# Summing the modulation vectors: from ones-matmuls and transposes on TensorE to block transposes and row sums on VectorE

## The chip, the cores and the metric

The kernel runs on one core of a Trainium2 chip. The metric is device time in microseconds (us), the median of several executions. The engines named below are TensorE (PE, with its weight loads as PEld), VectorE (DVE), ScalarE (ACT), GpSimd (POOL) and SyncE (SP), which here issues all the transfers from HBM.

## The reference, cut to what matters

Two layers of a diffusion backbone over 256 latent tokens and 256 context tokens, width 1024. Each layer is modulated by six vectors of 1024 numbers for each of the two streams (latent and context). They come from a product of one vector with a wide matrix:

```python
mod   = silu(c)     @ w_mod[l] + b_mod[l]      # (6144,) for the latent stream
mod_c = silu(c_ctx) @ w_mod[l] + b_mod[l]      # (6144,) for the context stream
sh1, sc1, gt1, sh2, sc2, gt2 = split(mod, 6)
h = rms_norm(x, g_norm1) * (1 + sc1) + sh1     # -> w_in, gates, attention, convolution, Fourier mixing
x = x + gt1 * merge_branches(...)              # -> w_o
x = x + gt2 * sq_relu_mlp(rms_norm(x, g_norm2) * (1 + sc2) + sh2)
```

The second layer leaves the context stream after its keys and values, so it needs two vectors of `mod_c` there and six of `mod`. Everything is float32.

## The kernel before, in words

Activations lie with the 1024 features on partitions (`xT`, 8 tiles of 128 features by 512 tokens). Every weight matrix is streamed from HBM once, in chunks of 1 MB (`raw`, two buffers), and each half chunk is split into a high part (`whi`, a cast on ACT, L384) and a low part (`wlo`, a subtraction on DVE, L385). Three matmuls then make one product of float32 accuracy (L473, L476, L478 in `fm`). The stages are named in the tiles: `init`, `n1L`, `uL`, `convL`, `fouL`, `qkvL`, `gateL`, `agL`, `woL`, `ffL`, once for each layer.

Beside this main work runs a side stream, the modulation vectors. For each of the six vectors and each half of it (512 columns, `j` and `h`), `mod_loads` fetches four transfers of 512 KB (`modr`, two buffers, L298), and `mod_steps` accumulates on DVE: `acc[p, n] = sum over k of cs[p, k] * w[128 k + p, n]`, one multiply (L349) and seven multiply-adds (L351) of 128x512 for each stream. What is left is the sum over the 128 partitions `p`, a turn of the 512 sums from a row onto partitions (the modulation is used as `modT[p, f]`, feature `128 f + p`), and the bias. That is `mod_finish`, called once for each pair of accumulators: two streams of one half vector, or two halves of one vector where only one stream is needed. There are 8 calls for layer 0 and 8 for layer 1, 16 in all.

`mod_steps` is a generator. Each `yield` in it is a step, and `fm` calls `mods.tick()` after each contraction tile, which takes 0.6, 1.3, 0.4 or 0.8 steps by stage (`RATES`). `mod_need` takes steps until a vector is ready, and `mods.drain()` takes all that are left before the end of layer 0. In `mod_finish` the steps `W1` and `W2` are pauses, so that the next instruction of the chain is written some tiles later. The final order on each engine is set by a scheduler, which simulates the program and places each instruction where its inputs are ready; instructions in `tc.keep_in_program_order` keep their order among themselves. All engines are in order once the program is built, so a late instruction holds what is behind it on its engine.

In the kernel before, a call does four matmuls with `ones` as weights of 32 columns, each on 256 columns of an accumulator and each into its own group of 32 partitions of one PSUM tile (L308), a copy on ACT (L313), two transposes of 128x128 on TensorE through a PSUM tile of the shared pool `aux` (L318), and two additions of the bias on DVE (L321).

Of the kernel before, what the change touches and what calls it, by code (L numbers as in the profile page):

```python
# [8 lines left out]
F32 = mybir.dt.float32  # L9
F32R = mybir.dt.float32r  # L10
AF = mybir.ActivationFunctionType
ALU = mybir.AluOpType
AX = mybir.AxisListType
PSUM = bass.MemoryType.PSUM

P = 128
# [14 lines left out]
W_INIT, W_RMS = 6, 6  # L31
MLAG = 1
LAG = 2
W1, W2 = 3, 2
RATES = [0.6, 1.3, 0.4, 0.8]
AR = [1.3, 0.8]

# [2 lines left out]
def hybrid_block_kernel(  # L40
# [7 lines left out]
    nc = tc.nc  # L48
    V = nc.vector
    A = nc.scalar  # L50
    G = nc.gpsimd
    PE = nc.tensor

    const = ctx.enter_context(tc.tile_pool(name="const", bufs=1))
# [7 lines left out]
    pmod = ctx.enter_context(tc.tile_pool(name="pmod", bufs=1, space=PSUM))  # L62
# [4 lines left out]
    def nm(s):  # L67
        uid[0] += 1
        return f"{stage[0]}_{s}_{uid[0]}"
# [4 lines left out]
    def scratch(shape=(P, 512), dt=F32):  # L74
        return scr.tile(list(shape), dt, tag="scr", name=nm("scr"))

    def small(shape, tag, dt=F32, bufs=4):
        return tiny.tile(shape, dt, tag=tag, name=nm(tag), bufs=bufs)

    def bank(shape=(P, 512)):  # L80
        return psum.tile(list(shape), F32, tag="mm", name=nm("mm"))

    def aux(shape=(P, 512)):
        return paux.tile(list(shape), F32, tag="aux", name=nm("aux"))
# [45 lines left out]
    ident = const.tile([P, P], F32, tag="ident", name="ident")  # L130
    make_identity(nc, ident)
    ones = const.tile([P, P], F32, tag="ones", name="ones")
    G.memset(ones, 1.0)
    mhalf = const.tile([P, 1], F32, tag="mhalf", name="mhalf")
    G.memset(mhalf, -0.5)
    cT = scratch((P, KT, 32))
# [10 lines left out]
    prm = []  # L147
# [38 lines left out]
    def accs(streams):  # L186
        t = const.tile([P, 4, 512], F32, tag="kT", name=nm("acc"))[:, 0, :]
        return [Acc(s * S, S, t) for s in streams]
# [62 lines left out]
    modT = [const.tile([P, 48, 2], F32, tag=f"modT{l}", name=f"modT{l}") for l in range(DEPTH)]  # L251
# [49 lines left out]

    def mod_finish(accs, dsts, l):

        ps = pmod.tile([P, 256], F32, tag="mod", name=nm("mod"))
        for _ in range(W1):
            yield
        for g in range(4):
            tc.keep_in_program_order(PE.matmul(  # L308
                ps[32 * g : 32 * g + 32, :], ones[:, 0:32],
                accs[g // 2][:, (g % 2) * 256 : (g % 2 + 1) * 256], start=True, stop=True,  # L310
            ))
        sb = scratch()[:, :256]
        A.copy(sb, ps)  # L313
        for _ in range(W2):
            yield
        tp = aux((P, 2, P))
        for e in range(2):
            tc.keep_in_program_order(PE.transpose(tp[:, e, :], sb[:, e * P : (e + 1) * P], ident))  # L318
        tv = tp.rearrange("p e (g r) -> p g e r", r=32)[:, :, :, 0]
        for i, (f, s) in enumerate(dsts):  # L320
            V.tensor_tensor(  # L321
                modT[l][:, f : f + 4, s].rearrange("p (g e) -> p g e", e=2),
                tv[:, 2 * i : 2 * i + 2, :],
                prm[l][:, f : f + 4].rearrange("p (g e) -> p g e", e=2), op=ALU.add,
            )
        yield

    ready = set()
# [5 lines left out]
    def mod_steps(todo):  # L334
        loads = mod_loads(todo)
        cur = next(loads, None)
        accs, dsts = [], []
        while cur is not None:
            l, j, ns, h, k2, r = cur
            cur = next(loads, None)  # L340
            if k2 == 0:
                for s in range(ns):
                    accs.append(small([P, 512], "acc", bufs=2))
                    dsts.append((j * 8 + h * 4, s))
            for kk in range(2):
                for s in range(ns):
                    a, w = accs[s - ns], cs2[:, s, 2 * k2 + kk : 2 * k2 + kk + 1]
                    if k2 + kk == 0:
                        v = V.tensor_scalar(a, r[:, kk, :], w, None, op0=ALU.mult)  # L349
                    else:  # L350
                        v = V.scalar_tensor_tensor(a, r[:, kk, :], w, a, op0=ALU.mult, op1=ALU.add)  # L351
                    tc.keep_in_program_order(v)
                    yield
            if k2 == KT // 2 - 1 and len(accs) == 2:
                yield from mod_finish(accs, dsts, l)
                accs, dsts = [], []
                if h == 1:
                    ready.add((l, j))
# [187 lines left out]
    for l in range(DEPTH):  # L546
# [69 lines left out]
        for ft in range(2):  # L616
            t = scratch()
# [15 lines left out]
        for ft in range(2):  # L633
# [4 lines left out]
            t = scratch()  # L638
# [31 lines left out]
        for tt in range(nt):  # L670
            ps = aux((P, 2, 256))
# [17 lines left out]
        for ft in range(2):  # L689
            ps = aux()  # L690
# [111 lines left out]
        for ci, c0 in ((2, OFF_K), (0, OFF_Q), (1, OFF_Q + 256)):  # L802
            ch = plain(w_in[l], 0, c0, (V, G) if last else (V, V)).prep()
            for tt in range(4 if ci == 2 else nt):
                ps = bank((P, 256))
                tk = slice(tt * P, (tt + 1) * P)
                for kt in range(KT):
                    wh, wl = ch.at(kt, 0, 256)
                    a, b = hh[:, kt, tk], hl[:, kt, tk]
# [122 lines left out]
        for j in range(4):  # L932
# [5 lines left out]
            for o in range(2):  # L938
                f = 2 * j + o
# [42 lines left out]
        acc = accs(streams)  # L982
# [50 lines left out]
        for b in range(nblk):  # L1033
            subs = []
            hot = None
            for q in range(2):
                hid = bigt([P, 2, per, T])
                subs.append(hid)
                for j in range(per // 2):
# [12 lines left out]
                    for o in range(2):  # L1052
                        t = scratch()[:, :T]
# [20 lines left out]
            if nr == 1:  # L1074
                if final and not last:
                    mods.drain()
                    acc = accs(streams)
# [17 lines left out]
            else:  # L1095

                nk = 2 * per
                for h in range(2):
# [14 lines left out]
                    for tt in range(2):  # L1113
                        t = scratch()
# [51 lines left out]
```

## Time and profile before

| what | value |
|---|---|
| median of 3 runs | 1146.95 us (1144.39 to 1149.06) |
| profiled execution: its time, its span | 1148.35 us, 1146.5 us |
| PE busy | 1127.0 us, 98% |
| DVE busy | 779.6 us, 68% |
| ACT busy | 504.4 us, 44% |
| DMA, over the span | 180 MB, 156 GB/s |
| granted TensorE clock | 0.996 of full speed |

Durations are those of one profiled execution. A PE row's time is that of one matmul from its start to its modelled end; matmuls overlap, so what a matmul costs is read from the distance between the starts around it. A float32 matmul that isn't split by the program shows as two records. The stages that hold the side stream lie between 131 us and 747 us of the span: `gateL` of layer 0 from about 131 us, `agL` from 285 us, `woL` from about 346 us, `ffL` from about 398 us.

### The profile page before, as it was taken

To read this page: it belongs to the slowest core of one execution; us is meant where nothing else is said; L and a number is where in the kernel's file an instruction comes from. 1 tells how busy PE (TensorE), PEld (TensorE's weight loads), DVE (VectorE), ACT (ScalarE), POOL (GpSimd) and SP (SyncE) were. 2 spreads that over 40 slices of the span, in tenths; PEclk is the share of its full clock that TensorE was granted. 3 is DMA by queue.
4 is the path that set the end of the run, shared out by engine and by line. 5 is a ranking of instruction groups with operands and counts; after the bars stand their busy time and mean duration, and the time that the engine had idled before them with its cause. 6 is when DMAs were issued, how large, how long until landed. Compare 5 with 4: busy or idle time off the path is not lost.

```text
span 1146.5 us, 17789 instructions
## 1 busy us (share of the span) xinstructions
PE 1127.0 (98%) x7075; PEld 983.9 (86%) x7075; DVE 779.6 (68%) x1444; ACT 504.4 (44%) x896; POOL 50.6 (4%) x54
## 2 busy tenths in 40 slices
PE   7899999999999999999999999999999999999998
PEld 6689887887787998878888888899999999988986
DVE  4577775568878876766746664778886567756754
ACT  4345544443332454143134135244666456754752
POOL 0002100000000100000000000043300000000000
PEclk9999999999999999999999999999999999999999
DMA  9933322225655243655456664515434465656653
GB/s 279 295 97 100 107 78 92 82 85 147 202 175 179 91 162 117 196 184 165 146 168 202 217 209 145 199 61 175 139 111 129 131 207 178 184 182 186 184 184 111
DMA packets 156796, 180.03 MB, mean 157 GB/s; under 512 B 5260, under 2 KB 126504, under 8 KB 156712
## 3 DMA queue, kind: packets, MB, share of 16 engines
q1 hardware_dynamic: 156712, 178.88, 50.1%
q8 instruction: 56, 0.92, 0.3%
q14 instruction: 28, 0.23, 0.1%
HBM read 177.81 MB, written 1.05 MB: 156 GB/s over the span
## 4 chain that ended last, share of the span: by engine, by line
PE 88%; DVE 4%; DMA 4%; SPq 2%; ACT 1%; issue 1%; POOL 1%; DVEq 0%; ACTq 0%; POOLq 0%
PE ffL_mm L473 12%; PE ffL_mm L476 12%; PE ffL_mm L478 12%; PE gateL_mm L478 5%; PE gateL_mm L473 5%; PE gateL_mm L476 5%; PE agL_mm L476 3%; PE agL_mm L473 3%; PE agL_mm L478 3%; PE ffL_mm L1112 3%; PE ffL_mm L1111 3%; PE ffL_mm L1110 3%; PE woL_mm L476 2%; PE woL_mm L478 2%; PE woL_mm L473 2%; SPq L105 2%
## 5 line engine op out<-in xcount | busy, mean ns | idle before, releaser
L384 ACT CAST ffL_whi<-ffL_raw 128x1024 fp32r<-128x1024 f32 x128 | 134.4, 1052 | 218.9 <-PE ffL_mm L478 164.3
L385 DVE TENSOR_TENSOR ffL_wlo<-ffL_raw,ffL_whi 128x1024 fp32r<-128x1024 f32 x127 | 155.0, 1222 | 99.3 <-ACT ffL_whi L384 99.1
L473 PE MATMUL ffL_mm<-woL_big,ffL_whi 128*128 128x258 f32 (+2 forms) x544 | 171.0, 329 | 0.0
L476 PE MATMUL ffL_mm<-woL_big,ffL_wlo 128*128 128x258 f32 (+2 forms) x544 | 170.5, 327 | 0.0
L478 PE MATMUL ffL_mm<-woL_big,ffL_whi 128*128 128x258 f32 (+2 forms) x544 | 133.2, 328 | 0.0
L473 PEld LDWEIGHTS ffL_mm<-woL_big,ffL_whi 128*128 128x128 f32 x544 | 103.1, 190 | 10.2 <-issue 1.6
L476 PEld LDWEIGHTS ffL_mm<-woL_big,ffL_wlo 128*128 128x128 f32 x544 | 103.1, 190 | 8.9 <-issue 0.4
L351 DVE SCALAR_TENSOR_TENSOR ffL_acc<-ffL_modr,cs,ffL_acc 128x512 f32<-128x512 f32 x126 | 90.4, 747 | 24.4 <-DMA ffL_modr<-in_w_mod_dram 23.4
L473 PE MATMUL ffL_mm<-ffL_big,ffL_whi 128*128 128x512 f32 (+1 forms) x288 | 105.4, 368 | 0.0
L476 PE MATMUL ffL_mm<-ffL_big,ffL_wlo 128*128 128x512 f32 (+1 forms) x288 | 104.9, 367 | 0.0
L478 PEld LDWEIGHTS ffL_mm<-woL_big,ffL_whi 128*128 128x128 f32 x544 | 91.0, 190 | 8.7
L478 PE MATMUL ffL_mm<-ffL_big,ffL_whi 128*128 128x512 f32 (+1 forms) x288 | 85.1, 367 | 0.0
L473 PEld LDWEIGHTS ffL_mm<-ffL_big,ffL_whi 128*128 128x128 f32 x288 | 54.3, 189 | 10.6 <-issue 2.1
L476 PEld LDWEIGHTS ffL_mm<-ffL_big,ffL_wlo 128*128 128x128 f32 x288 | 54.3, 189 | 9.1 <-issue 0.4
L385 DVE TENSOR_TENSOR gateL_wlo<-gateL_raw,gateL_whi 128x1024 fp32r<-128x1024 f32 x40 | 48.8, 1221 | 19.3 <-ACT gateL_whi L384 19.1
L478 PEld LDWEIGHTS ffL_mm<-ffL_big,ffL_whi 128*128 128x128 f32 x288 | 53.2, 189 | 8.7
L384 ACT CAST gateL_whi<-gateL_raw 128x1024 fp32r<-128x1024 f32 x40 | 42.0, 1051 | 22.0 <-PE gateL_mm L478 18.2
L476 PE MATMUL gateL_mm<-n1L_big,gateL_wlo 128*128 128x512 f32 x128 | 50.7, 396 | 0.0
L473 PE MATMUL gateL_mm<-n1L_big,gateL_whi 128*128 128x512 f32 x128 | 50.5, 396 | 0.0
L1110 PE MATMUL ffL_mm<-ffL_whi,ffL_big 128*128 128x512 f32 x128 | 49.9, 390 | 0.0
L1111 PE MATMUL ffL_mm<-ffL_wlo,ffL_big 128*128 128x512 f32 x128 | 49.8, 389 | 0.0
L1112 PE MATMUL ffL_mm<-ffL_whi,ffL_big 128*128 128x512 f32 x128 | 49.8, 389 | 0.0
(339 smaller groups left out, 2626.8 us busy)
## 6 DMA issues: line engine op xcount, KB each, us to landing
ffL_raw<-in_w_ff_dram SPq DMA_DIRECT2D x64, 1024.0 KB, 5.5
ffL_modr<-in_w_mod_dram SPq DMA_DIRECT2D x53, 512.0 KB, 4.3
gateL_raw<-in_w_in_dram SPq DMA_DIRECT2D x16, 1024.0 KB, 5.3
init_big<-in_w_mod_dram SPq DMA_DIRECT2D x16, 512.0 KB, 7.8
agL_raw<-in_w_in_dram SPq DMA_DIRECT2D x8, 1024.0 KB, 5.4
woL_raw<-in_w_o_dram SPq DMA_DIRECT2D x8, 1024.0 KB
qkvL_raw<-in_w_in_dram SPq DMA_DIRECT2D x6, 1024.0 KB
agL_modr<-in_w_mod_dram SPq DMA_DIRECT2D x11, 512.0 KB, 5.1
```

Source lines behind the costliest of these rows:

```text
L105: tc.keep_in_program_order(nc.sync.dma_start(dst, src))
L351: v = V.scalar_tensor_tensor(a, r[:, kk, :], w, a, op0=ALU.mult, op1=ALU.add)
L384: a = A.copy(hi[:, :n], src)
L385: b = eng.tensor_tensor(lo[:, :n], src, hi[:, :n].bitcast(F32), op=ALU.subtract)
L473: m = PE.matmul(d, wh, rh, start=kt == first, stop=False)
L476: PE.matmul(d, wl, rh, start=False, stop=False)
L478: PE.matmul(d, wh, rl, start=False, stop=kt == final)
L1110: PE.matmul(bs[tt], hid[:, 0], wh, start=kk == 0, stop=False)
L1111: PE.matmul(bs[tt], hid[:, 0], wl, start=False, stop=False)
L1112: PE.matmul(bs[tt], hid[:, 1], wh, start=False, stop=kk == nk - 1)
```

## The change

`mod_finish` now works on DVE up to the last sum. For each of the two accumulators it makes a block transpose of 128x512 (`V.transpose`: each 32x32 block is turned in place, so that `t[32 a + r, 32 b + c] = acc[32 a + c, 32 b + r]`) into a scratch tile, and sums over `c` into 16 columns of `red` (128 x 2 x 16). What is left is the sum over the four quadrants `a`, which one matmul makes: its weights `sel` hold a one wherever the two partition numbers agree modulo 32. Every quadrant of the result holds all the sums; four additions of the bias, on 32 partitions each, pick their columns from it. `sel` is built once, at the start. The matmul has 128 rows, 128 weight columns and 32 columns of data. A call is now 5 steps where it was 6: two with the transposes and sums, `W1` = 2 pauses, and the last. The copy on ACT and the use of the pool `aux` are gone. One line of the builder's arguments changes a scratch size for transfers issued by GpSimd, of which there are none here.

```diff
-W1, W2 = 3, 2
+W1 = 2
...
+    sel = const.tile([P, P], F32, tag="sel", name="sel")
+    quad = small([P, 32], "quad", bufs=1)
+    V.reduce_sum(quad, ident.rearrange("p (g c) -> p c g", c=32), axis=AX.X)
+    V.tensor_copy(sel.rearrange("p (g c) -> p g c", c=32), quad.unsqueeze(1).to_broadcast([P, 4, 32]))
...
     def mod_finish(accs, dsts, l):
-        ps = pmod.tile([P, 256], F32, tag="mod", name=nm("mod"))
+        red = small([P, 2, 16], "red", bufs=2)
+        for i, acc in enumerate(accs):
+            t = scratch()
+            tc.keep_in_program_order(V.transpose(t, acc))
+            tc.keep_in_program_order(
+                V.reduce_sum(red[:, i], t.rearrange("p (b r) -> p b r", r=32), axis=AX.X))
+            yield
         for _ in range(W1):
             yield
+        ps = pmod.tile([P, 2, 16], F32, tag="mod", name=nm("mod"))
+        tc.keep_in_program_order(PE.matmul(
+            ps.rearrange("p i b -> p (i b)"), sel, red.rearrange("p i b -> p (i b)"),
+            start=True, stop=True))
+        (f, s0), (_, s1) = dsts
         for g in range(4):
-            tc.keep_in_program_order(PE.matmul(
-                ps[32 * g : 32 * g + 32, :], ones[:, 0:32],
-                accs[g // 2][:, (g % 2) * 256 : (g % 2 + 1) * 256], start=True, stop=True,
-            ))
-        sb = scratch()[:, :256]
-        A.copy(sb, ps)
-        for _ in range(W2):
-            yield
-        tp = aux((P, 2, P))
-        for e in range(2):
-            tc.keep_in_program_order(PE.transpose(tp[:, e, :], sb[:, e * P : (e + 1) * P], ident))
-        tv = tp.rearrange("p e (g r) -> p g e r", r=32)[:, :, :, 0]
-        for i, (f, s) in enumerate(dsts):
-            V.tensor_tensor(
-                modT[l][:, f : f + 4, s].rearrange("p (g e) -> p g e", e=2),
-                tv[:, 2 * i : 2 * i + 2, :],
-                prm[l][:, f : f + 4].rearrange("p (g e) -> p g e", e=2), op=ALU.add,
-            )
+            q = slice(32 * g, 32 * g + 32)
+            src = ps[q].rearrange("p i (c g) -> p i c g", g=4)[:, :, :, g]
+            if s1 != s0:
+                dst = modT[l][q, f : f + 4, :].rearrange("p c i -> p i c")
+                bias = prm[l][q, f : f + 4].unsqueeze(1).to_broadcast([32, 2, 4])
+            else:
+                dst = modT[l][q, f : f + 8, s0].rearrange("p (i c) -> p i c", c=4)
+                bias = prm[l][q, f : f + 8].rearrange("p (i c) -> p i c", c=4)
+            V.tensor_tensor(dst, src, bias, op=ALU.add)
         yield
...
-    nc = bacc.Bacc("TRN2", target_bir_lowering=False, num_devices=1)
+    nc = bacc.Bacc("TRN2", target_bir_lowering=False, num_devices=1, dynamic_dma_scratch_size=1024)
```

Since the scheduler places every instruction anew, the order moves in many places from 190 us on. Three of them follow. Line numbers of the changed kernel are higher: by 5 up to L298 (now L303), by 10 behind `mod_finish` (L385 is L395, L473 is L483).

On PE, in `ffL` of layer 0, one call of `mod_finish` before: `ffL_mod` is the PSUM tile of the sums, `ffL_acc` the two accumulators, the other rows are the three-matmul products of the feed-forward weights.

```order
L478 MATMUL ffL_mm_5078<-ffL_big_4835,ffL_whi_5110 128x512
L478 MATMUL ffL_mm_5079<-ffL_big_4835,ffL_whi_5110 128x512
L308 MATMUL ffL_mod_5103<-ffL_acc_4903,ones 32x256 x2
L308 MATMUL ffL_mod_5103<-ffL_acc_4904,ones 32x256 x2
L473 MATMUL ffL_mm_5078<-ffL_big_4835,ffL_whi_5110 128x512
```

The same call in the changed kernel:

```order
L488 MATMUL ffL_mm_5097<-ffL_big_4854,ffL_whi_5130 128x512
L488 MATMUL ffL_mm_5098<-ffL_big_4854,ffL_whi_5130 128x512
L322 MATMUL ffL_mod_5140<-ffL_red_5087,sel 128x32
L483 MATMUL ffL_mm_5097<-ffL_big_4854,ffL_whi_5130 128x512
L486 MATMUL ffL_mm_5097<-ffL_big_4854,ffL_wlo_5131 128x512
```

Four matmuls became one, and the two transposes that stood 22 rows further down are gone. In 11 of the 16 calls before, the four stood together as here; in the other 5 they stood as two pairs, each behind its own accumulator, so that there were 21 such groups.

On DVE, the end of `agL` in layer 0 before, from the last gated product (L903) to the last low part of the merged branches (`agL_big`, L486), which the output projection `woL` reads on PE:

```order
L903 SCALAR_TENSOR_TENSOR agL_scr_3326<-agL_scr_3326,agL_mm_3333 128x512
L351 SCALAR_TENSOR_TENSOR agL_acc_3196<-agL_modr_3273,cs_110,agL_acc_3196 128x512
L903 SCALAR_TENSOR_TENSOR agL_scr_3328<-agL_scr_3328,agL_mm_3334 128x512
L351 SCALAR_TENSOR_TENSOR agL_acc_3197<-agL_modr_3273,cs_110,agL_acc_3197 128x512
L385 TENSOR_TENSOR woL_wlo_3544<-woL_raw_3507,woL_whi_3543 128x1024
L941 TENSOR_TENSOR agL_scr_3326<-agL_scr_3326,gateL_big_1468 128x512
L941 TENSOR_TENSOR agL_scr_3328<-agL_scr_3328,gateL_big_1468 128x512
L486 TENSOR_TENSOR agL_big_2854<-agL_scr_3326,agL_big_2853 128x512
L349 TENSOR_SCALAR woL_acc_3386<-agL_modr_3301,cs_110 128x512
L385 TENSOR_TENSOR woL_wlo_3595<-woL_raw_3588,woL_whi_3594 128x1024
L486 TENSOR_TENSOR agL_big_2854<-agL_scr_3328,agL_big_2853 128x512
```

And in the changed kernel, from one row ahead of the same gated products (now L913; the low parts are L496):

```order
L359 TENSOR_SCALAR agL_acc_3367<-agL_modr_3287,cs_114 128x512
L913 SCALAR_TENSOR_TENSOR agL_scr_3346<-agL_scr_3346,agL_mm_3353 128x512
L913 SCALAR_TENSOR_TENSOR agL_scr_3348<-agL_scr_3348,agL_mm_3354 128x512
L317 TENSOR_REDUCE agL_red_3315<-agL_scr_3325 128x16
L359 TENSOR_SCALAR agL_acc_3368<-agL_modr_3287,cs_114 128x512
L361 SCALAR_TENSOR_TENSOR agL_acc_3367<-agL_modr_3287,cs_114,agL_acc_3367 128x512
L395 TENSOR_TENSOR woL_wlo_3554<-woL_raw_3517,woL_whi_3553 128x1024
L951 TENSOR_TENSOR agL_scr_3346<-agL_scr_3346,gateL_big_1472 128x512
L951 TENSOR_TENSOR agL_scr_3348<-agL_scr_3348,gateL_big_1472 128x512
L361 SCALAR_TENSOR_TENSOR agL_acc_3368<-agL_modr_3287,cs_114,agL_acc_3368 128x512
L361 SCALAR_TENSOR_TENSOR agL_acc_3367<-agL_modr_3365,cs_114,agL_acc_3367 128x512
L496 TENSOR_TENSOR agL_big_2864<-agL_scr_3346,agL_big_2863 128x512
```

A row sum (L317) and more multiply-adds now stand between the gated products and the low parts. From the first gated product of `agL` to the first residual of `woL` the DVE's order holds 34 multiply-adds (L351) before and 38 now, and 5 block transposes, 6 row sums and 12 small additions (against 6 at L321) that were not there.

On SP, in `ffL`, one stretch of the queue before (L423 loads feed-forward weights, L298 modulation weights):

```order
L423 DMA ffL_raw_5552<-in_w_ff_dram 128x8x256
L423 DMA ffL_raw_5635<-in_w_ff_dram 128x8x256
L298 DMA ffL_modr_5455<-in_w_mod_dram 128x2x512
L298 DMA ffL_modr_5496<-in_w_mod_dram 128x2x512
L298 DMA ffL_modr_5516<-in_w_mod_dram 128x2x512
L298 DMA ffL_modr_5538<-in_w_mod_dram 128x2x512
L423 DMA ffL_raw_5711<-in_w_ff_dram 128x8x256
```

And the same three weight loads in the changed kernel:

```order
L433 DMA ffL_raw_5576<-in_w_ff_dram 128x8x256
L303 DMA ffL_modr_5479<-in_w_mod_dram 128x2x512
L303 DMA ffL_modr_5520<-in_w_mod_dram 128x2x512
L303 DMA ffL_modr_5541<-in_w_mod_dram 128x2x512
L433 DMA ffL_raw_5658<-in_w_ff_dram 128x8x256
L303 DMA ffL_modr_5563<-in_w_mod_dram 128x2x512
L303 DMA ffL_modr_5597<-in_w_mod_dram 128x2x512
L303 DMA ffL_modr_5690<-in_w_mod_dram 128x2x512
L433 DMA ffL_raw_5740<-in_w_ff_dram 128x8x256
```

The second weight load now stands behind three modulation loads that it had no need to pass before. Counted from the program's start, 50 modulation loads stood ahead of it, and now 55. Of the 32 feed-forward weight loads of this layer, 5 have three or more additional modulation loads ahead of them; none has fewer than before.

## The prediction

> **What bounds the kernel now.** I read the page's busy times first, then who waited for whom (PE from 60 us on: waiter, releaser, us in total, times, longest), then the busy times of the stretches in which the side stream runs (columns: stretch, length, then busy us of PE, PEld, DVE, ACT, POOL, clock, DMA share, GB/s).
>
> ```profile
> PE 1127.0 (98%) x7075; PEld 983.9 (86%) x7075; DVE 779.6 (68%) x1444; ACT 504.4 (44%) x896; POOL 50.6 (4%) x54
> ...
> PE fouL_aux L446 <- DVE fouL_big L486: 1.2, 1, 1.2
> ...
> PE ffL_mod L308 <- DVE ffL_acc L351: 0.4, 1, 0.4
> ACT ffL_whi L384 <- PE ffL_mm L478: 164.3, 60, 5.2
> ...
> 131.00:285.00 154.00, 154.00 (x884) 125.14 (x883) 101.98 (x198) 69.02 (x146) 0.00 (x0) 1.00 0.34 102
> 285.00:357.00 72.00, 72.00 (x327) 56.63 (x327) 58.48 (x87) 22.31 (x31) 0.00 (x0) 1.00 0.59 184
> 357.00:420.00 63.00, 63.00 (x476) 59.65 (x476) 51.01 (x102) 25.93 (x48) 3.89 (x3) 1.00 0.38 120
> 500.00:745.00 245.00, 244.62 (x1156) 199.63 (x1155) 157.12 (x240) 85.13 (x129) 0.00 (x0) 1.00 0.57 185
> sum 614.00, PE 613.62 PEld 505.40 DVE 423.45 ACT 230.64 POOL 3.89; mean PE 122.72 PEld 101.08 DVE 84.69 ACT 46.13 POOL 0.78
> ```
>
> The reader is to see that PE is never idle between 131 and 745 us but for 0.4 us, and that this is no artefact of overlapping matmuls alone: ACT, which makes the weights that PE uses next, waited 164.3 us in `ffL` for PE to free a buffer. The suppliers run ahead of PE. So a microsecond of PE work that disappears there is a microsecond of span, as long as DVE, which gets the work, keeps ahead. DVE is busy 66% of `gateL`, 64% of `ffL`, but 81% of `agL` and `woL` (285 to 420 us): that is where the danger lies.
>
> **What leaves PE.** Rows of PE in order of time (start, length, name, form, records): one call's four matmuls in `ffL`, and two transposes in `woL`; then the busy time of all L308 and of all L318 between 131 and 747 us, and that of L308 in `agL` alone.
>
> ```profile
> 625.82 0.39 PE L476 MATMUL ffL_mm<-ffL_big,ffL_wlo 128*128 128x512 f32 x1
> 626.04 0.39 PE L473 MATMUL ffL_mm<-ffL_big,ffL_whi 128*128 128x512 f32 x1
> 626.27 0.39 PE L476 MATMUL ffL_mm<-ffL_big,ffL_wlo 128*128 128x512 f32 x1
> 626.50 0.61 PE L478 MATMUL ffL_mm<-ffL_big,ffL_whi 128*128 128x512 f32 x2
> 627.04 0.64 PE L308 MATMUL ffL_mod<-ffL_acc,ones 128*32 128x256 f32 x8
> 627.61 0.50 PE L473 MATMUL ffL_mm<-ffL_big,ffL_whi 128*128 128x512 f32 x1
> 627.95 0.39 PE L476 MATMUL ffL_mm<-ffL_big,ffL_wlo 128*128 128x512 f32 x1
> ...
> 374.50 0.40 PE L478 MATMUL woL_mm<-agL_big,woL_whi 128*128 128x256 f32 x2
> 374.74 0.38 PE L318 MATMUL woL_aux<-ident,woL_scr 128*128 128x128 f32 x2
> 374.87 0.36 PE L473 MATMUL woL_mm<-agL_big,woL_whi 128*128 128x256 f32 x1
> 375.07 0.28 PE L476 MATMUL woL_mm<-agL_big,woL_wlo 128*128 128x256 f32 x1
> ...
> 131.00:747.00 616.00, 13.29 (x128) 1.00 0.49 155
> 131.00:747.00 616.00, 6.19 (x32) 1.00 0.49 155
> 285.00:357.00 72.00, 3.14 (x24) 0.73 (x24) 1.00 0.59 184
> ```
>
> Counting durations would mislead: the four matmuls are eight records that lie on top of each other, 0.64 us in all. The cost is read from the starts. From 625.82 to 626.50 three 512-column matmuls start, one each 0.227 us. From 626.50 to 627.95 there are again three (two L478, one L473), which should take 0.68 us and take 1.45: the group costs 0.77 us. All L308 together are busy 13.29 us; at 0.633 us a group that makes 21 groups, as the order has it (11 calls with four together, 5 with two pairs; a pair costs the same). So 21 x 0.77 = 16.2 us leave. The transposes: from 374.50 to 375.07 three starts of 256 columns at 0.12 us would take 0.36 and take 0.57; two transposes cost 0.21 us, 16 x 0.21 = 3.4 us.
>
> [...]
>
> **What comes to PE.** Sixteen float32 matmuls with 128x128 weights and 32 columns. The nearest row has the same weights and one column (two matmuls, four records):
>
> ```profile
> 383.83 0.28 PE L473 MATMUL woL_mm<-agL_big,woL_whi 128*128 128x256 f32 x1
> 383.95 0.50 PE L203 MATMUL woL_aux<-ones,woL_acc 128*128 128x1 f32 x4
> 384.32 0.36 PE L476 MATMUL woL_mm<-agL_big,woL_wlo 128*128 128x256 f32 x1
> 384.52 0.40 PE L478 MATMUL woL_mm<-agL_big,woL_whi 128*128 128x256 f32 x2
> ```
>
> From 383.83 to 384.52 two starts at 0.12 us should take 0.24 and take 0.69: 0.225 us a matmul, 16 x 0.225 = 3.6 us. Above, one alone could cost the 0.77 us of an L308 group (8.7 us more in all); I take the near row, since there too the weights fill all columns.
>
> **What comes to DVE.** No block transpose stands in the trace. Rows of DVE, one group each (count, busy us, mean ns):
>
> ```profile
> L351 DVE SCALAR_TENSOR_TENSOR agL_acc<-agL_modr,cs,agL_acc 128x512 f32<-128x512 f32 x28 | 19.6, 745 | 1.8 <-DMA agL_modr<-in_w_mod_dram 1.7
> L941 DVE TENSOR_TENSOR agL_scr<-agL_scr,gateL_big 128x512 f32<-128x512 f32 x8 | 5.4, 682 | 0.0
> L349 DVE TENSOR_SCALAR agL_acc<-agL_modr,cs 128x512 f32<-128x512 f32 x4 | 1.7, 477 | 0.0
> L385 DVE TENSOR_TENSOR agL_wlo<-agL_raw,agL_whi 128x1024 fp32r<-128x1024 f32 x6 | 7.3, 1219 | 5.9 <-ACT agL_whi L384 5.9
> L837 DVE TENSOR_REDUCE gateL_mx<-gateL_aux 128x1 f32<-128x512 f32 x32 | 21.8, 683 | 9.7 <-PE gateL_aux L834 9.6
> 328.57 0.22 DVE L321 TENSOR_TENSOR modT<-agL_aux,prm 128x4 f32<-128x4 f32 x2
> 292.04:358.61 66.57, 66.57 (x304) 52.11 (x303) 53.21 (x81) 20.29 (x28) 0.00 (x0) 1.00 0.56 175
> 358.61:440.00 81.39, 81.39 (x558) 74.62 (x560) 61.26 (x112) 36.95 (x66) 3.89 (x3) 1.00 0.42 136
> ```
>
> A row sum of 128x512 takes 0.68 us (L837). For the block transpose the bounds are the cheapest pass over 128x512, 1.7/4 = 0.43 us (L349), and a pass over twice as much, 1.22 us (L385); I take 0.68, the plain pass (L941). The small additions go at 0.11 us. A call then costs DVE 2 x 0.68 + 2 x 0.68 + 4 x 0.11 - 2 x 0.11 = 2.9 us more, 47 us in all (39 to 64). From 131 to 745 us DVE is idle for 614 - 423 = 191 us, so on average this is covered.
>
> [...]
>
> The tight place is `agL`, where 1.3 steps are taken per tile. Between the first gated product (292.04) and the first residual of `woL` (358.61) DVE was busy 53.21 us. The order adds 4 multiply-adds at 0.70, 11 passes at 0.68, 12 small additions less 6: 2.8 + 7.5 + 0.7 = 11.0 us, together 64.2. PE's work of 66.57 us loses 5 groups there (3.14 us busy at 0.633), 3.9 us, and the transposes and new matmuls cancel: 62.7 us. DVE ends 1.5 us late, and late next is the last `agL_big`, which `woL` reads: I add 1.5 us. With the transpose at its bounds it is 0.3 or 4.2 us. After 358.61 us the DVE has room again, 20 us idle up to 440 us in the trace.
>
> **The rest costs nothing.** ACT loses its copies, and it mostly waits:
>
> ```profile
> L313 ACT COPY ffL_scr<-ffL_mod x10: 366/373/376, 440.8 to 741.5; 128x256 f32<-128x256 f32 x10
> ```
>
> Sixteen at 0.37 us are 6 us of ACT, which the 164.3 us that ACT waits for PE make worthless. Building `sel` is two small DVE instructions while DVE waits for its first transpose. The new matmul waits for the last row sum, and all products of `fm` queue behind it on PE; before, L308 waited for the multiply-adds in the same way and lost 0.4 us in all, with the order placing both where their input is ready. I take nothing; at worst each of the 16 finds one long subtraction (1.22 us) ahead of its row sum, 19.5 us. SP's order is the third rival.
>
> **The sum.** -16.2 - 3.4 + 3.6 + 1.5 = -14.5 us. The profiled execution took 1148.35 us, so 1133.9; it lay 1.4 us above the median of the runs shown, 1146.95, and against that: 1132.5 us, -1.3%.
>
> **Rivals.** (1) DVE is late more often: the transpose at its upper bound, 4.2 us late at `woL` instead of 1.5, and some of the sixteen matmuls waiting, 0.3 us each on average, 4.8 us. Then 1132.5 + 2.7 + 4.8 = 1140. For it speaks the 81% in `agL` and `woL`; against it the 0.4 us of waits at L308 before. Chance 0.17.
>
> (2) The change doesn't speed PE up, because the new waits take the place of the old matmuls: each of the sixteen at the 1.22 us above, -14.5 + 19.5, 1152 us, or about 1147 if three quarters of it come. It needs an order that places every matmul too early for the chip. Against it: before, only one such wait in 21 was seen. Chance 0.12.
>
> (3) Slower, by SP. The weight loads of `ffL` share a queue with the modulation loads, and each of these waits for DVE to free one of two buffers:
>
> ```profile
> SPq L298 <- DVE ffL_acc L351: 118.3, 49, 10.1
> ffL_raw<-in_w_ff_dram SPq DMA_DIRECT2D x64, 1024.0 KB, 5.5
> ffL_modr<-in_w_mod_dram SPq DMA_DIRECT2D x53, 512.0 KB, 4.3
> ```
>
> Five weight loads get three to five more modulation loads ahead of them. SP's queue took 53 such loads over some 340 us of `ffL`, 6.4 us each: three are 19 us. A chunk lasts PE eight tiles of six matmuls at 0.227 us, 11 us, and lands in 5.5, so with the second buffer a load can be about 12 us late before PE sees it. Past that point the five cost 7 us each: 1132.5 + 35 = 1167. Against it: the modulation loads come earlier in the new order because their steps are written earlier, and DVE may free the buffers as early. Chance 0.07.
>
> **How the numbers follow.** The forecast has 0.64 (its own range 1129 to 1136). What a measurement tells from no change is 0.5%, 5.7 us: 1141.2 and 1152.7 us are the borders. Faster: 0.64 and 0.15 of rival 1, 0.79. Same: 0.02 and rival 2, 0.14. Slower: 0.07. The range 1128 to 1142 holds the forecast and rival 1, some 0.8; its lower end is the transpose at its lower bound, 1.2 us less, and the 2.5 us by which the fastest run lies under the median.
>
> **What would show it.** In the changed profile: PE's busy time down by about 16 us, and its waits for DVE between 131 and 745 us at 2 us or less, most of it at the `woL` product that reads the last `agL_big`; the new matmul at about 0.22 us between the starts around it; the block transpose near 0.68 us; DVE's busy time near 825 us. I am wrong if PE waits at the new matmul again and again (rival 2), or for `ffL_whi` behind a weight load (rival 3).

## The result and the profile after

The changed kernel takes 1132.63 us (median of 4 runs, 1131.46 to 1133.91) beside 1145.67 us for the kernel before in the same comparison: a ratio of 0.988, 95% interval 0.986 to 0.991. A second comparison gave 1132.72 beside 1146.65 us, 0.988 (0.986 to 0.990). The forecast was 1132.5 us, for a gain of 14.5; against the medians of the kernel before the gain is 13.0 us here and 13.9 in the second comparison.

The changed kernel's page, busy time and instructions of each engine; then its waits of PE from 60 us on (waiter, releaser, us in total, times, longest):

```profile
PE 1109.4 (98%) x6947; PEld 981.7 (87%) x6947; DVE 825.0 (73%) x1542; ACT 499.3 (44%) x880; POOL 49.8 (4%) x54
```

```profile
PE gateL_aux L859 <- DVE qkvL_big L853: 1.7, 1, 1.7
PE fouL_aux L456 <- DVE fouL_big L496: 1.6, 1, 1.6
PE ffL_aux L223 <- DVE ffL_scr L222: 1.3, 1, 1.3
PE woL_aux L223 <- DVE woL_scr L222: 0.9, 1, 0.9
PE woL_mm L483 <- ACT agL_big L495: 0.8, 1, 0.8
PE gateL_aux L859 <- ACT qkvL_big L861: 0.5, 1, 0.5
PE n1L_mm L488 <- DVE ffL_big L232: 0.3, 1, 0.3
```

PE is busy 17.6 us less, and its waits hold no row of L322, the new matmul. Its stretches, at borders near those that the prediction used (stretch, length, then busy us of PE, PEld, DVE, ACT, POOL, clock, DMA share, GB/s):

```profile
131.00:285.00 154.00, 151.82 (x868) 125.00 (x867) 107.78 (x208) 68.24 (x144) 0.00 (x0) 1.00 0.32 101
285.00:357.00 72.00, 72.00 (x322) 59.67 (x321) 68.15 (x109) 22.28 (x29) 0.00 (x0) 1.00 0.62 185
357.00:420.00 63.00, 62.06 (x469) 59.62 (x468) 57.12 (x111) 30.74 (x55) 3.88 (x3) 1.00 0.44 141
500.00:733.00 233.00, 232.92 (x1087) 194.80 (x1086) 169.10 (x273) 80.99 (x119) 0.00 (x0) 1.00 0.57 183
sum 602.00, PE 598.80 PEld 505.40 DVE 469.14 ACT 226.16 POOL 3.88; mean PE 119.76 PEld 101.08 DVE 93.83 ACT 45.23 POOL 0.78
```

DVE is busy 95% in `agL` now (68.15 of 72 us), and PE idle 3.2 us in these stretches (602.00 - 598.80) where before it was idle 0.4. The prices of the new instructions, by the rows of their lines (count, shortest/median/longest ns, first and last start, form), and one new matmul in PE's rows in order of time (start, length):

```profile
L315 DVE STREAM_TRANSPOSE ffL_scr<-ffL_acc x18: 671/702/709, 452.2 to 714.5; 128x512 f32<-128x512 f32 x18
```

```profile
L317 DVE TENSOR_REDUCE ffL_red<-ffL_scr x20: 639/678/686, 422.6 to 715.8; 128x16 f32<-128x512 f32 x20
```

```profile
433.37 0.62 PE L488 MATMUL ffL_mm<-woL_big,ffL_whi 128*128 128x512 f32 x2
433.82 0.30 PE L322 MATMUL ffL_mod<-ffL_red,sel 128*128 128x32 f32 x2
433.96 0.48 PE L483 MATMUL ffL_mm<-ffL_big,ffL_whi 128*128 128x512 f32 x1
434.27 0.39 PE L486 MATMUL ffL_mm<-ffL_big,ffL_wlo 128*128 128x512 f32 x1
434.50 0.40 PE L483 MATMUL ffL_mm<-ffL_big,ffL_whi 128*128 128x512 f32 x1
```

From 433.37 to 434.27 three starts of 512 columns, two L488 and one L483, would take 0.68 us and take 0.90: the new matmul costs 0.22 us, read at this one place.

One more view is needed to compare the two executions, the granted clock. Here is a stretch before the side stream begins, of the kernel before and then of the changed one:

```profile
58.00:66.00 8.00, 7.95 (x27) 6.11 (x28) 3.64 (x13) 1.34 (x3) 0.00 (x0) 0.79 0.00 2
```

```profile
58.00:66.00 8.00, 7.93 (x34) 6.24 (x35) 5.01 (x15) 2.90 (x6) 0.00 (x0) 1.00 0.00 2
```

In the execution before, PE ran these 8 us at 0.79 of its clock: 8 x 0.21 = 1.7 us of its busy time are slow clock, not work. So the spans compare as follows. Busy PE without that: 1127.0 - 1.7 = 1125.3 before, 1109.4 after, -15.9. The slow clock: -1.7. Idle PE: 1146.5 - 1127.0 = 19.5 before, 1132.1 - 1109.4 = 22.7 after, +3.2. Together -14.4, the difference of the two spans.

By stages (first row of PE in each, before and after):

| stage of layer 0 | before | after | gained so far |
|---|---|---|---|
| `gateL` | 126.3 | 124.8 | 1.5, the clock above |
| `agL` | 275.6 | 274.1 | 1.5 |
| `woL` | 343.9 | 339.9 | 4.0 |
| `ffL` | 393.5 | 387.7 | 5.8 |
| next layer, `n1L` | 758.7 | 744.0 | 14.7 |

Beside the gates nothing is gained: three groups of old matmuls (3 x 0.77 = 2.3 us) left, and 2.2 us of waits at L859 came, where PE now needs the normalised softmax before it is ready. Most of the gain is in `ffL`.

### The profile page after: what moved, and what is told of

It reads as the page before. It is cut to its first block, busy times and chain, and to the rows that moved or that the text cites. A ratio compares the mean times of both kernels' runs of the same rounds, so it can differ in the third digit from the quotient of the medians.

```text
span 1132.1 us, 17609 instructions
## 1 busy us (share of the span) xinstructions
PE 1109.4 (98%) x6947; PEld 981.7 (87%) x6947; DVE 825.0 (73%) x1542; ACT 499.3 (44%) x880; POOL 49.8 (4%) x54
## 4 chain that ended last, share of the span: by engine, by line
PE 87%; DMA 5%; DVE 3%; SPq 2%; ACT 1%; issue 1%; POOL 1%; ACTq 0%; DVEq 0%; POOLq 0%
PE ffL_mm L483 13%; PE ffL_mm L488 13%; PE ffL_mm L486 13%; PE gateL_mm L483 5%; PE gateL_mm L488 5%; PE gateL_mm L486 5%; PE ffL_mm L1122 3%; PE ffL_mm L1121 3%; PE ffL_mm L1120 3%; PE agL_mm L488 2%; PE agL_mm L483 2%; PE agL_mm L486 2%; SPq L105 2%; PE gateL_aux L844 2%; PE gateL_aux L871 2%; DMA convL_raw<-in_w_in_dram 2%
## 5 line engine op out<-in xcount | busy, mean ns | idle before, releaser
L395 DVE TENSOR_TENSOR ffL_wlo<-ffL_raw,ffL_whi 128x1024 fp32r<-128x1024 f32 x127 | 155.0, 1221 | 69.6 <-ACT ffL_whi L394 69.6
L483 PE MATMUL ffL_mm<-woL_big,ffL_whi 128*128 128x258 f32 (+2 forms) x544 | 170.7, 328 | 0.1
L486 PE MATMUL ffL_mm<-woL_big,ffL_wlo 128*128 128x258 f32 (+2 forms) x544 | 170.4, 327 | 0.0
L488 PE MATMUL ffL_mm<-woL_big,ffL_whi 128*128 128x258 f32 (+2 forms) x544 | 132.7, 327 | 0.0
L483 PEld LDWEIGHTS ffL_mm<-woL_big,ffL_whi 128*128 128x128 f32 x544 | 103.0, 190 | 9.3 <-issue 0.7
L486 PEld LDWEIGHTS ffL_mm<-woL_big,ffL_wlo 128*128 128x128 f32 x544 | 103.1, 190 | 8.5
L483 PE MATMUL ffL_mm<-ffL_big,ffL_whi 128*128 128x512 f32 (+1 forms) x288 | 105.1, 367 | 0.0
L486 PE MATMUL ffL_mm<-ffL_big,ffL_wlo 128*128 128x512 f32 (+1 forms) x288 | 104.7, 366 | 0.0
L488 PEld LDWEIGHTS ffL_mm<-woL_big,ffL_whi 128*128 128x128 f32 x544 | 91.0, 190 | 8.8
L488 PE MATMUL ffL_mm<-ffL_big,ffL_whi 128*128 128x512 f32 (+1 forms) x288 | 84.5, 366 | 0.0
L486 PEld LDWEIGHTS ffL_mm<-ffL_big,ffL_wlo 128*128 128x128 f32 x288 | 54.3, 189 | 8.6
L395 DVE TENSOR_TENSOR gateL_wlo<-gateL_raw,gateL_whi 128x1024 fp32r<-128x1024 f32 x40 | 48.9, 1222 | 17.8 <-ACT gateL_whi L394 17.6
L483 PEld LDWEIGHTS ffL_mm<-ffL_big,ffL_whi 128*128 128x128 f32 x288 | 54.3, 189 | 8.6
L488 PEld LDWEIGHTS ffL_mm<-ffL_big,ffL_whi 128*128 128x128 f32 x288 | 53.2, 189 | 8.8
L486 PE MATMUL gateL_mm<-n1L_big,gateL_wlo 128*128 128x512 f32 x128 | 50.4, 394 | 0.0
L483 PE MATMUL gateL_mm<-n1L_big,gateL_whi 128*128 128x512 f32 x128 | 50.2, 394 | 0.0
```

Of the source, the lines that this page charges most:

```text
L395: b = eng.tensor_tensor(lo[:, :n], src, hi[:, :n].bitcast(F32), op=ALU.subtract)
L483: m = PE.matmul(d, wh, rh, start=kt == first, stop=False)
L486: PE.matmul(d, wl, rh, start=False, stop=False)
L488: PE.matmul(d, wh, rl, start=False, stop=kt == final)
```

## Experiments

All times are medians. The comparison's own ratio to the kernel before, with its interval, stands with each.

**Is it PE's time, and is it paid per group?** First, the changed kernel with the old matmuls back, whose results nothing reads (code cut to what differs, here and below):

```
 ps (now pm[:, 256:288]) ...
+for g in range(4):
+    PE.matmul(pm[32*g : 32*g+32, 0:256], ones[:, 0:32],
+              accs[g // 2][:, (g % 2)*256 : (g % 2 + 1)*256], ...)
 PE.matmul(ps, sel, red)
```

> The changed kernel, and in each call the four matmuls with 32 columns of ones are done as well, from the same accumulators into a free part of the same PSUM tile; nothing reads them. The program's order has 23 groups of them. Theory: 23 x 0.77 = 17.7 us on PE come back, 1149 to 1152 us, PE busy about 14.5 us higher (23 x 0.633), near 1124 us. Rival (the gain came from the freed PSUM buffers, the copy on ScalarE or the pacing, not from PE time): 1133 to 1137 us.

Measured: 1149.07 us, ratio 1.002 (1.000 to 1.004).

```profile
PE 1126.0 (98%) x7075; PEld 983.7 (86%) x7075; DVE 825.6 (72%) x1542; ACT 498.3 (43%) x880; POOL 49.7 (4%) x54
```

The whole gain is gone with these matmuls alone, while the VectorE passes, the missing copy and transposes, the five steps a call and the builder's argument stay as in the change. 16.4 us over the 1132.7 us of the change are 0.71 us for each of 23 groups (0.67 if each kernel is taken against the kernel before of its own comparison); PE's busy time rose by 16.6 us, 0.72 a group.

Second, the kernel before with the four matmuls of a call set apart:

```
-W1, W2 = 3, 2
+W1, W2 = 1, 1
 for g in range(4):
     PE.matmul(ps[32*g : 32*g+32, :], ones[:, 0:32], ...)
+    if g < 3:
+        yield
```

> The kernel before, with a step taken between the four matmuls of a call (W1 = 1, W2 = 1, so that a call still has six steps). The order then has 40 groups of L308 in place of 21: 24 of one matmul, 12 of two, 4 of four. Theory (the 0.77 us are paid per group, most of it where the narrow weights give way to full ones, whatever the number of matmuls in it): 1145.7 + 19 x 0.77 = 1160 us. Rival (paid per matmul, 0.25 us each, 64 in both): 1145 to 1147 us.

Measured: 1161.48 us beside 1147.55, ratio 1.012 (1.009 to 1.015).

```profile
PE 1141.4 (98%) x7075; PEld 984.2 (85%) x7075; DVE 779.7 (67%) x1444; ACT 503.9 (43%) x896; POOL 50.6 (4%) x54
```

The same 64 matmuls in 40 groups in place of 21 take 13.9 us more, 0.73 a group (busy: 14.4, 0.76 a group). The price is one of the group, near the 0.77 us read from the starts; a price per matmul would have left the time where it was. Why a group costs it (the narrow weights giving way to full ones, as the expectation had it) is not shown.

**What do VectorE's passes cost?** The changed kernel without them (so it leaves out the sums over partitions):

```
-t = scratch(); V.transpose(t, acc)
-V.reduce_sum(red[:, i], t as (16, 32))
+V.tensor_copy(red[:, i], acc[:, 0:16])
```

> The changed kernel, where each transpose and row sum is replaced by a copy of 16 columns of the accumulator; the sums over partitions are thus left out, the four-quadrant matmul reads other numbers, and its rows wait for the copy instead of the row sum. Theory: PE work as in the change, VectorE work near that of before the change (about 780 us): what VectorE's passes cost comes back, 1129 to 1131 us. Rival (passes cost nothing on the path): 1132 to 1133 us. Rival (passes cost much, balanced by chance): 1125 us or less.

Measured: 1129.04 us, ratio 0.986 (0.984 to 0.988). The interval overlaps that of the change, so 3.6 us is the best value and not a proven one. The profile says where it is:

```profile
PE 1108.6 (98%) x6947; PEld 980.2 (87%) x6947; DVE 790.8 (70%) x1510; ACT 498.3 (44%) x880; POOL 49.7 (4%) x54
```

PE is idle 1125.5 - 1108.6 = 16.9 us in place of 22.7 (21.3 in a second profile of the change), and all three waits of the change between 131 and 733 us are gone.

The kernel before, with the passes added and nothing reading them:

```
 ps = pmod.tile([P, 256], ...)
+for i, acc in enumerate(accs):
+    t = scratch(); V.transpose(t, acc)
+    V.reduce_sum(red[:, i], t as (16, 32))
+    yield
-for _ in range(W1):
+for _ in range(W1 - 2):
     yield
```

> The kernel before, and in each call the change's two block transposes and two row sums are done on VectorE as well; nothing reads their result. Still six steps. Theory: DVE busy up by 16 x 2.8 = 44 us to about 824 us, nearly all of it covered, 2 to 4 us late around the gates, agL and woL; 20 groups of L308 in place of 21 give 0.8 us back: 1147 to 1150 us. Rival (the added VectorE work costs more than was seen and the removed PE work was worth more, the two balancing by chance): 1155 us or more, at least 10 us over the kernel before. Rival (wholly free): 1145 us.

Measured: 1154.6 us, ratio 1.0067 (1.0049 to 1.0086): 8.5 us, twice what was expected and under the 10 of the rival. Its waits, three of the rows that the kernel before does not have, and a stretch just behind the start of `ffL`:

```profile
PE ffL_mm L480 <- ACT woL_big L240: 1.8, 1, 1.8
PE agL_mod L315 <- DVE agL_acc L358: 1.8, 1, 1.8
PE gateL_aux L856 <- DVE qkvL_big L850: 1.7, 1, 1.7
```

```profile
394.00:404.00 10.00, 8.46 (x56) 8.26 (x57) 8.79 (x22) 4.53 (x11) 0.70 (x1) 0.83 0.65 211
```

PE idles 5.9 us more (25.4 against 19.5), and right behind one of the waits the granted clock falls to a mean of 0.83 over 10 us, a loss of 1.7 us. The expectation had no such second price. Between the two profiled executions (1153.0 and 1146.5 us) it makes no difference, since the one of the kernel before lost the same 1.7 us at 58 to 66 us; over all runs the granted clocks are 0.9963 in the mean here and 0.9985 for the kernel before beside it, worth 0.0022 x 1150 = 2.5 of the 8.5 us.

The changed kernel with each pass done twice:

```
+for _ in range(2):
     t = scratch(); V.transpose(t, acc)
     V.reduce_sum(red[:, i], t as (16, 32))
```

> The changed kernel with each block transpose and row sum done twice (two transposes and two row sums for each accumulator; the second sum writes the same numbers). VectorE gets 44 us more, about 870 us in all. Theory: ffL has the room (169 of 233 us busy, and some 20 us come), agL and woL have not (68 of 72 us busy, about 7 us come): 3 to 8 us slower than the change, 1136 to 1141 us, all of it in waits between 285 and 420 us. Rival (VectorE is already near the bound everywhere): 1150 us or more. Rival (cover left everywhere): 1133 us.

Measured: 1156.58 us, ratio 1.007 (1.004 to 1.009): 24 us over the change, and the theory's 3 to 8 is wrong. Its longest waits, and three stretches of it:

```profile
PE agL_mod L323 <- DVE agL_red L318: 4.1, 1, 4.1
PE ffL_mod L323 <- DVE ffL_red L318: 3.5, 2, 3.0
PE woL_mm L484 <- ACT agL_scr L909: 1.7, 1, 1.7
```

```profile
262.00:276.00 14.00, 10.86 (x52) 8.23 (x49) 11.26 (x20) 4.56 (x12) 0.00 (x0) 0.76 0.38 112
352.00:364.00 12.00, 8.07 (x24) 6.55 (x25) 11.90 (x24) 2.27 (x3) 0.00 (x0) 0.72 0.28 91
530.00:542.00 12.00, 9.16 (x28) 7.42 (x29) 11.83 (x24) 1.35 (x2) 0.00 (x0) 0.72 0.41 129
```

In the profiled executions the difference is 20.3 us. PE idles 32.6 us against 22.7, 9.9 more. The rest is clock: 14 x 0.24, 12 x 0.28 and 12 x 0.28 are 3.4 us each, 10.2 us. The theory had put all of it in waits between 285 and 420 us. Only one of the three places lies there; the end of the gates (262 to 276 us) and `ffL` (530 to 542 us) were not as safe as it said, and the clock, half of the price, was missing.

Can more time for the new matmul's input take that away? The same kernel with `W1 = 5` in place of 2:

> The changed kernel with every block transpose and row sum done twice, as in the run that took 1156.6 us, and with W1 = 5 in place of 2, so that the four-quadrant matmul has three steps more for its input. Theory A (what the doubled passes cost there was waits, of which those at the four-quadrant matmul were 7.6 us, and after three of the waits a stretch of some 6 us at half the granted clock, 3.4 us each): the waits at L323 go and with them two of the three slow stretches, 1141 to 1147 us. Theory B (VectorE is simply out of throughput): the same 44 us of work has to be done, 1154 to 1158 us.

Measured: 1173.8 us, ratio 1.024 (1.023 to 1.026), so both theories miss. Its longest waits, and the two stretches in which they lie:

```profile
PE ffL_mod L323 <- DVE ffL_red L318: 11.8, 1, 11.8
PE woL_aux L208 <- DVE woL_acc L188: 7.3, 1, 7.3
PE woL_mod L323 <- DVE woL_red L318: 3.3, 1, 3.3
```

```profile
393.00:405.00 12.00, 1.42 (x8) 1.29 (x7) 11.54 (x26) 4.34 (x13) 0.00 (x0) 0.67 0.70 218
765.00:777.00 12.00, 1.20 (x11) 1.00 (x9) 9.95 (x15) 4.75 (x11) 5.49 (x2) 0.68 0.57 186
```

PE stands nearly still for 12 us twice, at the end of `woL` and at the end of the layer, while DVE works. The cause is in the program: three steps more in each of 16 calls make the side stream longer, and what is left of it is emitted in one lump at each place that needs its vectors. Counted as the program is built, these are the steps left where `woL` needs vectors 3 and 4, where `ffL` needs vector 5 behind the first of its four blocks, and where `mods.drain()` takes the rest at the end of the layer:

```
                       vectors 3, 4   vector 5   drain
before                     23            25        21
before, W1 = 2             17            23        13
after                      17            23        13
after, W1 = 3              23            25        21
after, W1 = 0               5            19         0
passes twice               17            23        13
passes twice, W1 = 5       35            29        37
RATES 0.7 1.0 0.5 0.9      24            19         0
RATES 0.5 1.1 0.4 0.9      35            21         0
```

The two stretches are the lumps of 35 and of 37 steps. So this run does not tell A from B: it made the lumps longer. What it shows is their price.

**Is it the shorter call?** The kernel before with `W1 = 2` (five steps), and the changed one with `W1 = 3` (six steps):

> The kernel before with W1 = 2 in place of 3: a call takes five steps, as in the change, and everything else stays. The program's order has 22 groups of L308 matmuls in place of 21. Theory (the gain is PE time of the L308 groups and transposes): 1146 to 1148 us, the kernel before plus one group of 0.77 us, with 2 us either way for a moved order; PE busy near 1127 us. Rival (the gain comes from the shorter call, which brings every modulation load and weight load earlier, and a new order): 1133 us, all or most of the gain.

Measured: 1150.7 us, ratio 1.0036 (1.0019 to 1.0053): 4.6 us slower, where the theory said 0 to 2 and the rival a gain of 13. The pacing alone gains nothing.

> The changed kernel with W1 = 3 in place of 2: six steps a call, as before the change. Theory (PE time): 1131 to 1135 us, PE busy near 1109 us. Rival (pacing): back to 1144 to 1147 us.

Measured: 1138.56 us, ratio 0.993 (0.991 to 0.995): 5.9 us slower than the change, in the middle between both expectations. The kernel before with five steps, and the change with six, each at the end of the gates:

```profile
262.00:270.00 8.00, 5.87 (x49) 3.89 (x50) 5.38 (x11) 4.20 (x12) 0.00 (x0) 0.91 0.53 139
270.00:278.00 8.00, 7.53 (x26) 5.39 (x23) 6.11 (x14) 2.47 (x6) 0.00 (x0) 0.66 0.45 136
```

```profile
262.00:270.00 8.00, 5.04 (x25) 3.72 (x26) 6.67 (x13) 3.83 (x10) 0.00 (x0) 0.63 0.54 151
270.00:278.00 8.00, 8.00 (x36) 6.59 (x35) 5.41 (x13) 1.05 (x1) 0.00 (x0) 0.94 0.01 2
```

Both lose 8 x 0.09 + 8 x 0.34, or 8 x 0.37 + 8 x 0.06, that is 3.4 us by the clock, behind waits of 2.7 and 3.2 us at that place. The kernel before with five steps has these waits without any added VectorE work: the order brings the softmax late there, not the passes. What this is worth has to be set against what the kernel beside it lost. For the five steps the two profiled executions differ by 2.1 us: 1.7 of clock (3.4 against 1.7) and 0.4 of idle time; the added group of 0.77 us isn't seen in busy time less slow clock. The other 2.5 of the medians' 4.6 us stay open: the granted clocks of all runs, 0.9976 in the mean against 0.9985, make 1.0 us. For the six, the clock and 0.5 us more idle time are 3.9 of 5.9 us (3.6 in the profiled executions). The runs' own clocks, 0.9947 in the mean of six against 0.9986 in the eight of the change, make 0.0039 x 1137 = 4.4 us, so much of the rest is likely clock too.

And the changed kernel with `W1 = 0`:

> The changed kernel with W1 = 0: the four-quadrant matmul is emitted right behind the step of the last row sum, three steps a call. Theory: the program's order is made by due times and places the matmul where its input is expected, so little changes: 1131 to 1136 us. Rival (the margin of two steps is what kept PE from waiting): up to 1.2 us for each of 16 matmuls, 1140 to 1152 us, with rows of PE at L322 in the waits.

Measured: 1135.8 us, ratio 0.989 (0.987 to 0.991). Its longest wait:

```profile
PE agL_mm L483 <- ACT agL_scr L908: 2.9, 1, 2.9
```

PE waits nowhere at L322, so the margin of two steps isn't what kept rival 2 away. The profiled execution is 3.5 us longer than that of the change, nearly all by the clock: 1.7 us behind this wait in `agL`, on ScalarE's gate, and 1.7 us before 70 us, ahead of the side stream. Idle time is the same (22.8 against 22.7): the two waits of the change in `woL` (0.9 and 0.8) are gone, and PE idles 1.2 us less before 58 us.

**A better version?** The changed kernel with other rates of the side stream (`RATES`), and the changed kernel itself beside them:

> The changed kernel itself, timed beside the kernel before and the others of this set. Theory and rivals alike: 1131 to 1134 us, mean granted clock 1.00 but for the start and the end.

Measured: 1132.72 us, ratio 0.988 (0.986 to 0.990).

> The changed kernel with RATES = [0.7, 1.0, 0.5, 0.9]: more of the side stream beside the gates, where VectorE was busy 70%, less in agL, where it was busy 95%. A call in search of a better version. If what is left of VectorE's price sits in agL and woL (0.9 us of waits seen there): 1131 to 1133 us. If a new order alone moves waits about, as the runs with five and six steps suggest: anything from 1130 to 1140 us, with waits of PE that its profile names.

Measured: 1142.55 us, ratio 0.996 (0.995 to 0.998).

> The changed kernel with RATES = [0.5, 1.1, 0.4, 0.9]: less beside the gates, where 2.2 us of waits on the softmax stood in the changed kernel, less in agL, more in ffL, where VectorE was busy 73%. If those 2.2 us come from VectorE's load beside the gates: 1130 to 1132 us. If a new order alone moves waits about: 1130 to 1140 us.

Measured: 1148.67 us, ratio 1.002 (1.000 to 1.004), the gain all gone. Neither is better. The longest waits of the even rates, then of the late ones, and the late ones' stretch around `woL`'s end:

```profile
PE ffL_mm L488 <- DVE ffL_big L496: 2.5, 1, 2.5
PE gateL_aux L859 <- DVE gateL_rs L852: 2.1, 1, 2.1
```

```profile
PE woL_aux L208 <- DVE woL_acc L188: 4.9, 1, 4.9
PE woL_aux L223 <- DVE woL_scr L222: 2.6, 1, 2.6
```

```profile
386.00:404.00 18.00, 9.43 (x48) 8.94 (x47) 17.08 (x42) 6.10 (x14) 1.07 (x1) 0.62 0.55 176
```

The late rates leave 35 steps for the place where `woL` needs its vectors, 17 in the change: DVE is busy 17.08 of 18 us, PE idles half of it, and 18 x 0.38 = 6.8 us pass as slow clock. The even rates leave 24 there; most of what they lose is clock (6.9 us in the table below).

**All runs together.** PE's busy and idle time in the profiled execution, and what slow clock took from it (the length of each 10 us stretch times one minus its granted clock, without the first and the last 20 us, where PE waits for loads and stores); the median beside it:

| kernel | PE busy | slow clock | busy less it | PE idle | median |
|---|---|---|---|---|---|
| before | 1127.0 | 1.7 | 1125.3 | 19.5 | 1145.7 to 1147.6 |
| before, five steps | 1128.7 | 3.4 | 1125.3 | 19.9 | 1150.7 |
| before, four apart | 1141.4 | 1.7 | 1139.7 | 19.8 | 1161.5 |
| before, passes added | 1127.6 | 1.7 | 1125.9 | 25.4 | 1154.6 |
| change, ones back | 1126.0 | 0 | 1126.0 | 21.2 | 1149.1 |
| change | 1109.4 | 0 | 1109.4 | 22.7 | 1132.6 |
| change, again | 1110.3 | 1.7 | 1108.6 | 21.3 | 1132.7 |
| change, no passes | 1108.6 | 0 | 1108.6 | 16.9 | 1129.0 |
| change, W1 = 0 | 1112.8 | 3.4 | 1109.4 | 22.8 | 1135.8 |
| change, six steps | 1112.5 | 3.4 | 1109.1 | 23.2 | 1138.6 |
| change, even rates | 1117.0 | 6.9 | 1110.1 | 24.0 | 1142.6 |
| change, late rates | 1116.8 | 8.6 | 1108.2 | 32.3 | 1148.7 |
| change, passes twice | 1119.8 | 10.2 | 1109.6 | 32.6 | 1156.6 |
| passes twice, W1 = 5 | 1119.5 | 22.2 | 1097.3 | 52.9 | 1173.8 |

But for two rows, PE's work falls into two levels, with the old matmuls (1125 to 1126) and without (1108 to 1110), whatever else is changed; the other differences are idle time and clock. The two rows are the matmuls set apart, which were to add work, and the last, where much of the slow clock lies in time in which PE stands still, so that it can't be taken off the busy time.

## Why the prediction was right, and where it was not

- **What leaves PE and what comes.** The terms 16.2 + 3.4 - 3.6 = 16.0 us stand against 15.9 us of busy time less slow clock. The group's 0.77 us came out as 0.67 to 0.76 in two runs built to ask it, so the first term may be 1 us too large or so (21 x 0.72 = 15.1). The transposes' 0.21 us a pair was not measured alone; it stands in the sum only. The new matmul took 0.22 us at the place read, as said.
- **The new VectorE work.** The block transpose took 0.70 us (0.68 was chosen between 0.43 and 1.22), the row sum 0.68, and DVE's busy time is 825.0 us, as forecast. That the total fits is in part luck: doing the 64 passes a second time raised the busy time by 37.2 us, adding them to the kernel before by 35.7, where the sum had 32 x 1.36 = 43.5, since records of neighbours overlap (a block transpose of 0.71 us starts at 452.18 us, the row behind it at 452.81); and the small additions take 10.35 us in all (before 3.64), 6.7 more where the sum had 3.5.
- **DVE late by 1.5 us.** This term was too small and had the wrong place: PE idles 3.2 us more over the whole span, and in the side stream's stretches it idles 2.2 us at the end of the gates and 0.9 at `woL`'s norm. The forecast put most of it at the last `agL_big` and bounded the waits at 2 us. `agL`, where DVE's room was worked out as 62.7 us for 64.2 us of work, ran at 95% and lost nothing. The runs that took the passes away, added them and doubled them agree that their price is in waits and in the slow clock that can follow them. It is not in proportion to the work: the same passes are worth 3.6 us in the change (best value), 8.5 in the kernel before, and 24 when done a second time.
- **"The rest costs nothing".** Here a step was left out: five steps a call in place of six leave shorter lumps, 17 steps in place of 23 where `woL` needs its vectors and 13 in place of 21 at the layer's end. Whether that helped is not shown. The runs with 35 show that a lump is not free; but the kernel before with five steps has the same 17 and 13 and gained nothing, and the change with `W1 = 0` has 5 and 0 and is 3 us slower.
- **The level.** The difference in the profiled executions, 14.4 us, holds 1.7 us of slow clock that happened to lie in the execution before. It was not in the sum, and the 1.5 us of late DVE were 1.7 us too few: the two cancel, so that 14.5 was met by luck within a tenth, though PE's 16.0 was not luck. The time was met within 0.1 us for one more such reason: the median of the kernel before came out at 1145.67 us with one run more, 1.3 us below the 1146.95 that the forecast started from, and the gain in medians was 13.0 to 13.9 us.
- **The rivals.** Rival 2 (waits at each new matmul) and rival 3 (weight loads behind modulation loads) did not happen: no wait at L322, none of PE for a load behind 60 us. Rival 1 (DVE late more often) was nearer than its 0.17: changed in its steps or in the rates, the same kernel takes 1136 to 1149 us, with waits of PE on VectorE and ScalarE and slow clock behind them. The sum was right because PE's part came out nearly the same in these orders (1108.2 to 1110.1 us of busy time less slow clock); that this order has so few waits was not foreseen but met.

## What to carry to other kernels

On a bound PE, price a small matmul by the starts around its group: a narrow one among full ones cost some 0.7 us a group, and one of full width 0.22. That part of the forecast held here whatever the order (1108.2 to 1110.1 us of busy time less slow clock, but for the run with `W1 = 5`); the part that the receiving engine pays didn't, so look for the places where a side stream is emitted in a lump and where the receiver has little room left, and count the waits there with the clock that they may cost (1.7 us or a multiple of it in these profiles). When a stream's length or rate changes, count again what is left over at each place that needs its result.

## What was not expected of the hardware

A slower granted clock began in or behind waits of PE of 1.8 us (the passes added to the kernel before, 393 to 396 us), 2.2 us (the change again, 261 to 265 us), 2.9 us (`W1 = 0`, 308 to 311 us) and 4.1 us (the passes done twice, 352 to 356 us), and the losses came in portions. The change with six steps, and the second profile of the changed kernel, at the same place:

```profile
264.00:268.00 4.00, 2.61 (x19) 1.91 (x19) 3.53 (x7) 1.34 (x4) 0.00 (x0) 0.52 0.63 145
268.00:272.00 4.00, 4.00 (x12) 3.20 (x13) 2.45 (x4) 1.38 (x3) 0.00 (x0) 0.63 0.33 117
272.00:276.00 4.00, 4.00 (x20) 3.35 (x19) 2.75 (x8) 0.64 (x1) 0.00 (x0) 1.00 0.00 0
```

```profile
264.00:268.00 4.00, 3.67 (x21) 2.94 (x22) 3.96 (x8) 2.61 (x6) 0.00 (x0) 0.59 0.80 199
268.00:272.00 4.00, 4.00 (x19) 3.27 (x18) 2.01 (x5) 0.00 (x0) 0.00 (x0) 0.99 0.16 60
```

The first loses 4 x 0.48 + 4 x 0.37 = 3.4 us, the second 4 x 0.41 + 0.04 = 1.7 us; the losses seen in these profiles are 1.7 us or, within a few tenths, multiples of it (1.7, 3.4, 6.8), as if stretches of 3.4 us, by estimate from 1.7 / 0.5, ran at half clock (in both, the clock is 0.50 from 266 to 268 us). The second has the same two waits there (1.7 and 0.5 us) as the first profile of the same kernel, which lost nothing. The same 2.2 us of waits, in two pieces with one transpose between them, stood ahead of a loss in one execution and not in the other. What decides it, no run here was built to show.
